# Input products of both feed-forwards of a decoder layer as seven block products each, with the weight block sums formed by GpSimd

## The chip, the cores and the metric

The kernel runs on one core of one Trainium2 chip. The metric is the device time of one execution in microseconds (us); the median of three timed executions of the kernel before is 1368.93 us, with 1367.86 and 1369.23 as lowest and highest.

The engines are named as the profile names them: PE is TensorE (matmuls), PEld its weight load, DVE is VectorE, ACT is ScalarE, POOL is GpSimd, SP is SyncE, which here issues the weight DMAs. SBUF is the memory that the engines work in, PSUM the accumulators that PE writes. Each engine takes its instructions in the order in which they stand in its own queue; a waiting instruction holds up those behind it.

## The reference

One layer for 512 tokens of 1024 features in float32: feed-forward, mixer (state-space heads beside differential attention), cross-attention to a memory, second feed-forward, final norm. The change touches both feed-forwards:

```python
def rms_norm(x, w):
    x32 = x.astype(jnp.float32)
    y = x32 * lax.rsqrt(jnp.mean(x32 * x32, axis=-1, keepdims=True) + EPS)
    return y.astype(x.dtype) * w

def swiglu(h, w_in, w_out):
    gate, up = jnp.split(h @ w_in, 2, axis=-1)
    return (jax.nn.silu(gate) * up) @ w_out

...
        x = x + 0.5 * swiglu(rms_norm(x, norm_ffn1_w[l]), ffn1_w_in[l], ffn1_w_out[l])
...
        x = x + 0.5 * swiglu(rms_norm(x, norm_ffn2_w[l]), ffn2_w_in[l], ffn2_w_out[l])
    return rms_norm(x, norm_final_w)
```

`w_in` is 1024 x 5632: 22 tiles of 128 columns for the gate and 22 for the up part.

## The kernel before

**Layout.** The state `x` lies feature-major: eight tiles `x[k]` of 128 features by 512 tokens. A product's weight tile (128 features by 128 outputs) is PE's stationary operand, the 512 tokens are the moving one, and the sum over the eight feature tiles is taken in one PSUM bank of 128 x 512.

**Three matmuls for one.** Every float32 operand is split into a rounded part and the rest (`hi` and `lo`, type fp32r): ACT writes `hi` (L144), DVE writes `lo = src - hi` (L145). `mm3` then takes hi x hi, hi x lo and lo x hi. A weight tile is thus loaded by `load_w` (L161): a 512 KB DMA into `wr` (128 x 1024, four buffers), ACT's `wh`, DVE's `wl` (three buffers each). At the start the splits of these weights are held by `tc.issue_after` until the splits of the first input tiles have been put in the queues (`start`).

**Feed-forward.** `ffn` (L289) goes through the 22 output tiles in three thirds of 8, 8 and 6. For each tile `ffn_pairs` (L270) makes the gate product `pg` and the up product `pu`, 8 x 3 matmuls each. DVE multiplies `pg` by the norm's row (L308), ACT takes the tanh (L310), DVE finishes the gate (L311) and multiplies by `pu` (L312), and the result is split into `g`. After a third, its `g` tiles go through eight output products `po` and are added to `x`. The first two tile pairs of the first feed-forward are special: `ffn_first` (L279) makes them together, one input tile at a time, as `x` and the first weights `wa` arrive. The norm's own row is ready only after that, and the gates wait for it. The last third of the second feed-forward is closed by token (`Close`, products `pf`), with the final norm; it loads its own weights through the same four `wr` buffers (`Close.weights`).

**What sets the order.** `Order` emits the matmuls: dense work is a queue of generators, and chains of dependent steps are let in after an estimated time (`od.t`). The tile framework's scheduler then sets the order of the queues of PE, DVE, ACT and POOL from this; only SP's queue stands as written. The framework also gives each new tile a free buffer of its pool and adds the waits for its release.

**The middle of the kernel** (mixer and cross-attention) isn't touched. It holds the only stage that runs matmuls of 256 columns back to back with a weight load each: `pck`, the keys of the memory (256 rows), in `memory_keys`.

## Time and profile before

| | us |
|---|---|
| median of three timed executions | 1368.93 |
| the profiled execution, its span | 1368.1 |
| PE busy | 1347.8 |
| DVE busy | 794.1 |
| ACT busy | 537.7 |
| POOL busy | 73.7 |

The profiled execution's own time is its span, 1368.1 us from the first to the last instruction, 0.8 us under the median. Shares and groups are for the whole span; the stages differ. In 60 to 370 us, which is nearly all of the first feed-forward, DVE is busy 153.97 of 310 us, ACT 88.50, POOL 3.08, and PE 310.00. A matmul's time in a row (390 ns for 512 columns) is from its start to the modelled end of its pipeline; the rate is read from the distance of starts, or from a piece of the chain of waits (its length over its count). The same holds in a lesser degree for DVE and ACT: the next instruction starts some 0.08 us ahead of the shown end of the one before.

### The profile page before, as it was taken

How to read it: one execution, taken by the hardware profiler on the slowest of the kernel's cores; microseconds unless marked ns; L12 is line 12 of the kernel's file. 1: busy time of each engine (PE TensorE's matmuls, PEld its weight loads, DVE VectorE, ACT ScalarE, POOL GpSimd, SP SyncE). 2: the span in 40 equal slices, each digit the busy share in tenths (PEclk: the TensorE clock that was granted, in tenths of full speed). 3: DMA queues.
4: the chain of work that ended last, by engine and by line, in shares of the span. 5: the costliest groups of instructions: out<-in, count | busy, mean ns of one | idle time of the engine just before them, and what ended most of it. 6: DMA issues, size and time to landing. Idle time of an engine off the chain costs nothing.

```text
span 1368.1 us, 16518 instructions
## 1 busy us (share of the span) xinstructions
PE 1347.8 (99%) x6457; PEld 1107.6 (81%) x6457; DVE 794.1 (58%) x1302; ACT 537.7 (39%) x958; POOL 73.7 (5%) x92
## 2 busy tenths in 40 slices
PE   8999999999999999999999989999999999999997
PEld 6888888888887788877888868888888888888886
DVE  6644444445786686657777767555654444444543
ACT  5421222223454564446654564343432222221432
POOL 1100000000020001100102111000000000000000
PEclk9999999999999999999999999999999999999999
DMA  6353333322342214432156274221323332332411
GB/s 237 110 164 113 94 93 99 100 92 81 115 154 65 91 47 100 125 91 70 29 142 104 80 148 137 94 63 47 92 93 96 104 94 93 103 112 77 136 50 62
DMA packets 41934, 136.74 MB, mean 100 GB/s; under 512 B 5552, under 2 KB 5960, under 8 KB 41856
## 3 DMA queue, kind: packets, MB, share of 16 engines
q1 hardware_dynamic: 37968, 124.61, 29.1%
q0 software_dynamic: 3888, 11.09, 4.9%
q8 instruction: 50, 0.82, 0.2%
q14 instruction: 28, 0.23, 0.1%
HBM read 133.52 MB, written 4.77 MB: 101 GB/s over the span
## 4 chain that ended last, share of the span: by engine, by line
PE 95%; DMA 1%; issue 1%; POOL 1%; ACT 1%; DVE 1%; SPq 0%; POOLq 0%; ACTq 0%; DVEq 0%
PE pg L135 17%; PE pu L135 17%; PE po L135 16%; PE pm L135 9%; PE pxbc L135 7%; PE pk L135 3%; PE pq L135 3%; PE pz L135 3%; PE pcq L135 3%; PE pv L135 3%; PE pf L135 2%; PE pa L135 2%; PE ps L135 2%; PE pck L135 1%; DMA wr<-in_wcv 1%
## 5 line engine op out<-in xcount | busy, mean ns | idle before, releaser
L144 ACT ACTIVATE wh<-wr 128x1024 fp32r<-128x1024 f32 (+2 forms) x228 | 232.6, 1022 | 546.6 <-issue 311.8
L145 DVE TENSOR_TENSOR wl<-wr,wh 128x1024 fp32r<-128x1024 f32 (+2 forms) x228 | 268.4, 1178 | 73.5 <-ACT wh L144 72.5
L135 PE MATMUL pg<-hmh,wl 128*128 128x512 f32 x336 | 130.9, 390 | 0.5 <-DVE wl L145 0.5
L135 PE MATMUL pg<-hmh,wh 128*128 128x512 f32 x336 | 131.1, 390 | 0.0
L135 PE MATMUL pu<-hmh,wh 128*128 128x512 f32 x336 | 131.0, 390 | 0.0
L135 PE MATMUL pg<-hml,wh 128*128 128x512 f32 x336 | 130.9, 390 | 0.0
L135 PE MATMUL pu<-hml,wh 128*128 128x512 f32 x336 | 130.8, 389 | 0.0
L135 PE MATMUL pu<-hmh,wl 128*128 128x512 f32 x336 | 130.8, 389 | 0.0
L135 PE MATMUL po<-gh,wh 128*128 128x512 f32 x304 | 118.4, 390 | 0.0
L135 PE MATMUL po<-gh,wl 128*128 128x512 f32 x304 | 118.3, 389 | 0.0
L135 PE MATMUL po<-gl,wh 128*128 128x512 f32 x304 | 118.3, 389 | 0.0
L312 DVE TENSOR_TENSOR gate<-pu,gate 128x512 f32<-128x512 f32 x42 | 29.0, 692 | 107.1 <-PE pu L135 107.1
L323 DVE TENSOR_TENSOR upd<-po,row 128x512 f32<-128x512 f32 x40 | 27.7, 692 | 98.3 <-PE po L135 98.2
L308 DVE TENSOR_TENSOR gate<-pg,row 128x512 f32<-128x512 f32 x42 | 29.0, 691 | 94.4 <-PE pg L135 94.4
L135 PEld LDWEIGHTS pg<-hmh,wl 128*128 128x128 f32 x336 | 63.1, 188 | 14.1 <-DVE wl L145 0.9
L135 PEld LDWEIGHTS pu<-hmh,wh 128*128 128x128 f32 x336 | 63.1, 188 | 13.9 <-issue 0.9
L135 PEld LDWEIGHTS pu<-hmh,wl 128*128 128x128 f32 x336 | 63.1, 188 | 13.2
L135 PEld LDWEIGHTS pg<-hmh,wh 128*128 128x128 f32 x336 | 63.1, 188 | 13.0
L135 PEld LDWEIGHTS pu<-hml,wh 128*128 128x128 f32 x336 | 63.1, 188 | 12.9
L135 PEld LDWEIGHTS pg<-hml,wh 128*128 128x128 f32 x336 | 63.1, 188 | 12.9
L135 PEld LDWEIGHTS po<-gh,wl 128*128 128x128 f32 x304 | 57.1, 188 | 12.0
L135 PEld LDWEIGHTS po<-gh,wh 128*128 128x128 f32 x304 | 57.1, 188 | 11.8
(310 smaller groups left out, 2704.8 us busy)
## 6 DMA issues: line engine op xcount, KB each, us to landing
wr<-in_f2i SPq DMA_DIRECT2D x44, 512.0 KB, 3.5
wr<-in_f1i SPq DMA_DIRECT2D x40, 512.0 KB, 3.5
wr<-in_f2o SPq DMA_DIRECT2D x22, 512.0 KB, 3.6
wr<-in_f1o SPq DMA_DIRECT2D x16, 512.0 KB, 3.6
wr<-in_wxbc SPq DMA_DIRECT2D x16, 512.0 KB, 3.6
wr<-in_wck SPq DMA_DIRECT2D x8, 512.0 KB, 3.5
wr<-in_wq SPq DMA_DIRECT2D x8, 512.0 KB, 3.8
wr<-in_wk SPq DMA_DIRECT2D x8, 512.0 KB, 3.5
```

What stands on the lines that cost most here:

```text
L135: nc.tensor.matmul(out, w, x, start=start, stop=stop)
L144: S.activation(hi, src, AF.Copy),
L145: V.tensor_tensor(lo, src, hi.bitcast(F32), ALU.subtract),
L308: V.tensor_tensor(gate, pg, st.row, ALU.mult)
L312: V.tensor_tensor(gate, pu, gate, ALU.mult)
L323: V.tensor_tensor(upd, po, row4, ALU.mult)
```

## The change

Four blocks are taken from the input and four from the weights, and the 2 x 2 block product is made with seven products in place of eight (Strassen's scheme in Winograd's form).

- **Input blocks** are even and odd feature tiles by first and second half of the tokens (`H` = 256 columns). `block_sums` forms the four sums S1 to S4 of a pair of tiles on DVE (two scalings of 512 columns, four sums of 256), then splits them (two ACT, two DVE instructions of 512): once in each feed-forward for each of four pairs.
- **Weight blocks** of a *quad* (two gate tiles and two up tiles): `b11` and `b21` are the gate's even and odd rows, `b12` and `b22` the up part's; each is 128 x 1024, one 512 KB DMA. POOL forms four sums t1 to t4 of them in SBUF (`sum_w`, `wt`, two buffers), and seven operands instead of four go through the ACT and DVE split.
- **Products.** `add_product` makes one block product: two output tiles, four pairs of feature tiles, three matmuls, each of 256 columns: 24 matmuls. A quad has seven: b11, t1, t2, b21, t3, b22, t4.
- **Combination.** Three PSUM banks `qa`, `qe`, `qb` hold the running sums. ACT copies `qa` into `qb` after the first product, keeps `p5` and `u2`; DVE subtracts `u2` from `qe` and makes `c22`. At the end `qa` and `qb` are the gate for the two halves of the tokens, `qe` and `c22` the up part.
- `ffn_quads` turns a quad into two `g` tiles (two gate chains of 512 columns, four multiplications of 256). The first feed-forward has 10 quads behind `ffn_first`, the second 11. A third has 3, 4, 3 and 4, 4, 3 quads.
- Four matmuls on a constant (`init`) are put at the start of PE's queue.
- The weights' layout in HBM is changed to match. Weights of quads are split by `split_w`, which has no `issue_after`.

```diff
+    def block_sums(k0, gain, raw):
+        fe, fo = s2("fe"), s2("fo")
+        V.tensor_scalar(fe, x[k0], par[:, gain + k0 : gain + k0 + 1], None, ALU.mult)
+        V.tensor_scalar(fo, x[k0 + 1], par[:, gain + k0 + 1 : gain + k0 + 2], None, ALU.mult)
+        s12, s34 = s2("s12"), s2("s34")
+        V.tensor_tensor(s12[:, :H], fe[:, H:], fo[:, H:], ALU.subtract)
+        V.tensor_tensor(s34[:, :H], fe[:, :H], fe[:, H:], ALU.subtract)
+        V.tensor_tensor(s12[:, H:], s12[:, :H], fe[:, :H], ALU.subtract)
+        V.tensor_tensor(s34[:, H:], s12[:, H:], fo[:, :H], ALU.add)
+        s12, s34 = split("s12", s12), split("s34", s34)
...
+    def add_product(ps, w, xs, which, first):
+        wh, wl = w
+        n = len(xs)
+        for f in range(2):
+            out = ps[:, f * H : (f + 1) * H]
+            for kp in range(n):
+                wc = slice((f * n + kp) * P, (f * n + kp + 1) * P)
+                xh, xl = xs[kp][which]
+                for j, (a_, b_) in enumerate(((wh, xh), (wh, xl), (wl, xh))):
+                    od.t += (H + 32) / 2400
+                    nc.tensor.matmul(out, a_[:, wc], b_, start=first and f == 0 and kp == 0 and j == 0, stop=kp == n - 1 and j == 2, skip_group_check=True)
+                yield
+
+    def raw_w(src):
+        raw = wp.tile([P, D], F32, tag="wr", name=nm("wr"), bufs=4)
+        nc.sync.dma_start(raw, src)
+        return raw
+
+    def sum_w(a_, b_):
+        t = wp.tile([P, D], F32, tag="wt", name=nm("wt"), bufs=2)
+        G.tensor_tensor(t, a_, b_, ALU.add)
+        return t
+
+    def split_w(raw):
+        hi = wp.tile([P, D], R32, tag="wh", name=nm("wh"))
+        lo = wp.tile([P, D], R32, tag="wl", name=nm("wl"))
+        split_into(hi, lo, raw)
+        return hi, lo
+
+    def quad(xs, src):
+        b12, b11 = raw_w(src[0]), raw_w(src[1])
+        a_ps = acc("qa")
+        yield from add_product(a_ps, split_w(b11), xs, "11", True)
+        t1 = sum_w(b11, b12)
+        e_ps = acc("qe")
+        b_ps = acc("qb")
+        S.activation(b_ps, a_ps, AF.Copy)
+        yield from add_product(e_ps, split_w(t1), xs, S1, True)
+        p5 = s2("p5")
+        S.activation(p5, e_ps, AF.Copy)
+        b22 = raw_w(src[2])
+        t2 = sum_w(t1, b22)
+        yield from add_product(b_ps, split_w(t2), xs, S2, False)
+        u2 = s2("u2")
+        S.activation(u2, b_ps, AF.Copy)
+        V.tensor_tensor(e_ps, e_ps, u2, ALU.subtract)
+        b21 = raw_w(src[3])
+        yield from add_product(a_ps, split_w(b21), xs, "12", False)
+        t3 = sum_w(b12, b22)
+        yield from add_product(b_ps, split_w(t3), xs, S3, False)
+        c22 = s2("c22")
+        V.tensor_tensor(c22, p5, b_ps, ALU.subtract)
+        yield from add_product(e_ps, split_w(b22), xs, S4, False)
+        t4 = sum_w(t2, b21)
+        yield from add_product(b_ps, split_w(t4), xs, "22", False)
+        yield (a_ps, b_ps), (e_ps, c22)
...
+    for _ in range(4):
+        nc.tensor.matmul(acc("init"), ones_r, ones_r[:, None, :].to_broadcast([P, 4, P]), start=True, stop=True)
...
-    def ffn_pairs(h, wi, f0, nf):
-        for f in range(f0, f0 + nf):
-            pg = acc("pg")
-            yield from proj(pg, load_w(wi[f]), h)
-            pu = acc("pu")
-            yield from proj(pu, load_w(wi[NF + f]), h)
-            yield pg, pu
...
+    def ffn_quads(xs, wq, st, nq, g):
+        for _ in range(nq):
+            made = None
+            for made in quad(xs, next(wq)):
+                if made is None:
+                    yield
+            gs, us = made
+            gates = []
+            for i in range(2):
+                row = st.row[:, None, i * H : (i + 1) * H].to_broadcast([P, 2, H])
+                gate = s2("gate")
+                V.tensor_tensor(halves(gate), halves(gs[i]), row, ALU.mult)
+                th = s2("th")
+                S.activation(th, gate, AF.Tanh, scale=0.5)
+                V.scalar_tensor_tensor(gate, th, 1.0, gate, ALU.add, ALU.mult)
+                gates.append(gate)
+            for f in range(2):
+                gf = s2("gf")
+                fs = slice(f * H, (f + 1) * H)
+                for i in range(2):
+                    V.tensor_tensor(gf[:, i * H : (i + 1) * H], us[i][:, fs], gates[i][:, fs], ALU.mult)
+                g.append(split("g", gf))
+            yield
...
             if ti == 0 and first is not None:
-                parts = [ffn_first(h, first), ffn_pairs(h, wi, f0 + 2, nf - 2)]
+                for made in ffn_first(h, first):
+                    if made is None:
+                        yield
+                    else:
+                        g.append(split("g", gated(*made, st.row)))
+                for k0 in range(0, KT, 2):
+                    xs.append(block_sums(k0, C_FFN1, h))
+                nq -= 1
...
     def upd_2(o, po):
         V.tensor_tensor(x[o], x[o], po, ALU.add)
         h_2.append(make_h(o, C_FFN2))
+        if o % 2:
+            xs_2.append(block_sums(o - 1, C_FFN2, h_2))
```

**How the queues stand.** Three places matter below. In the rows a name's last number counts tiles, and the number after the `L` is the line in the kernel whose queue it is.

First, DVE at the start of the first feed-forward, from the gate of the second tile pair of `ffn_first` (`pa`) on. Before, the gate of the next pair (`pg`) follows:

```order
L308 TENSOR_TENSOR gate_67_365<-pa_50_232,row_61_351 128x512
L145 TENSOR_TENSOR wl_90_482<-wr_88_479,wh_89_481 128x1024
L311 SCALAR_TENSOR_TENSOR gate_67_365<-th_68_367,gate_67_365 128x512
L312 TENSOR_TENSOR gate_67_365<-pa_52_234,gate_67_365 128x512
L145 TENSOR_TENSOR gl_70_372<-gate_67_365,gh_69_371 128x512
L308 TENSOR_TENSOR gate_79_437<-pg_71_375,row_61_351 128x512
```

Now the block sums stand there:

```order
L361 TENSOR_TENSOR gate_70_371<-pa_54_240,row_65_359 128x512
L364 SCALAR_TENSOR_TENSOR gate_70_371<-th_71_373,gate_70_371 128x512
L366 TENSOR_TENSOR gate_70_371<-pa_56_242,gate_70_371 128x512
L144 TENSOR_TENSOR wl_128_591<-wt_126_588,wh_127_590 128x1024
L144 TENSOR_TENSOR gl_73_378<-gate_70_371,gh_72_377 128x512
L180 TENSOR_SCALAR fe_74_381<-x0_79,par_77 128x512
L181 TENSOR_SCALAR fo_75_382<-x1_83,par_77 128x512
L183 TENSOR_TENSOR s12_76_385<-fe_74_381,fo_75_382 128x256
L184 TENSOR_TENSOR s34_77_386<-fe_74_381 128x256
L185 TENSOR_TENSOR s12_76_385<-s12_76_385,fe_74_381 128x256
L186 TENSOR_TENSOR s34_77_386<-s12_76_385,fo_75_382 128x256
L144 TENSOR_TENSOR s12l_79_392<-s12_76_385,s12h_78_391 128x512
```

The split of `s34` and three more such groups of eight, for the other pairs of input tiles, come right behind, all ahead of any further weight split.

Second, DVE and ACT where one quad ends and the next is under way. Before, for one output tile, DVE has:

```order
L308 TENSOR_TENSOR gate_199_1168<-pg_191_1106,row_61_351 128x512
L145 TENSOR_TENSOR wl_210_1213<-wr_208_1210,wh_209_1212 128x1024
L311 SCALAR_TENSOR_TENSOR gate_199_1168<-th_200_1170,gate_199_1168 128x512
L312 TENSOR_TENSOR gate_199_1168<-pu_195_1137,gate_199_1168 128x512
L145 TENSOR_TENSOR wl_218_1254<-wr_216_1251,wh_217_1253 128x1024
L145 TENSOR_TENSOR gl_202_1175<-gate_199_1168,gh_201_1174 128x512
```

Now, from the weight split for t1 of the next quad (`wl_354`), with `qb_314`, `qe_313` and `c22_329` from the quad that ends:

```order
L144 TENSOR_TENSOR wl_354_2028<-wt_350_2022,wh_353_2027 128x1024
L383 TENSOR_TENSOR gate_337_1970<-qb_314_1778,row_65_359 128x512
L392 TENSOR_TENSOR gf_339_1975<-qe_313_1777,gate_335_1965 128x256
L144 TENSOR_TENSOR wl_359_2062<-wt_357_2059,wh_358_2061 128x1024
L386 SCALAR_TENSOR_TENSOR gate_337_1970<-th_338_1972,gate_337_1970 128x512
L392 TENSOR_TENSOR gf_339_1975<-c22_329_1905,gate_337_1970 128x256
L144 TENSOR_TENSOR wl_363_2095<-wr_361_2092,wh_362_2094 128x1024
L144 TENSOR_TENSOR gl_341_1979<-gf_339_1975,gh_340_1978 128x512
```

And on ACT at the same place, where `qb_352` is the next quad's accumulator, copied from its `qa_347`:

```order
L385 ACTIVATE th_338_1972<-gate_337_1970 128x512
L143 ACTIVATE wh_362_2094<-wr_361_2092 128x1024
L143 ACTIVATE gh_340_1978<-gf_339_1975 128x512
L237 ACTIVATE qb_352_2025<-qa_347_1993 128x512
L143 ACTIVATE gh_343_1985<-gf_342_1982 128x512
```

The copy into `qb`, on which the next quad's third product rests, stands behind a step of the ended quad's gates.

Third, POOL within the feed-forwards. Before, it has only DMA issues and a few small things there (`mem` is the memory input):

```order
L215 TENSOR_TENSOR ncol_55_326<-nv_54_324,mhalf_120 128x4
L226 TENSOR_TENSOR ndiag_60_348<-ident_111,cl_57_342 128x512
L743 DMA mem_383_2292<-in_memT 128x256
L375 DMA rel_d_224<-rel_far_120_659 8x128
L743 DMA mem_386_2311<-in_memT 128x256
```

Now it has t1 to t4 of one quad, and then t1 and t2 of the next:

```order
L215 TENSOR_TENSOR wt_350_2022<-wr_346_1991,wr_345_1989 128x1024
L215 TENSOR_TENSOR wt_357_2059<-wt_350_2022,wr_356_2057 128x1024
L215 TENSOR_TENSOR wt_364_2122<-wr_345_1989,wr_356_2057 128x1024
L215 TENSOR_TENSOR wt_370_2182<-wt_357_2059,wr_361_2092 128x1024
L215 TENSOR_TENSOR wt_388_2269<-wr_384_2238,wr_383_2236 128x1024
L215 TENSOR_TENSOR wt_395_2306<-wt_388_2269,wr_394_2304 128x1024
```

With two `wt` buffers, t3 is written where t1 lay and so waits for DVE's split of t1, and t4 waits for the split of t2.

More of the change, by code (lines that the diff above doesn't have):

```diff
@@ L1 @@
 from contextlib import ExitStack
-from itertools import chain
 import math
@@ L233, in __init__ @@
             self.acc = None
+            self.row = None
         def add(self, xk):
@@ L938, in finish @@
                 nc.sync.dma_start(a["out"][tb][:, T:], xg[1])
-    od.add(ffn(h_2, st_2, a["f2i"], [a["f2o0"], a["f2o1"]], close=Close()))
+    od.add(ffn(h_2, xs_2, st_2, a["f2q"], [a["f2o0"], a["f2o1"]], close=Close()))
     od.run()
```

59 lines of the change are left out of this document (39 added, 20 removed).

## The prediction

> **What bounds the kernel now.** I read the page's busy line and the shares of the chain of waits first, then the chain in order of time inside the feed-forwards, then the timelines of DVE, ACT and POOL there.
>
> ```profile
> PE 1347.8 (99%) x6457; PEld 1107.6 (81%) x6457; DVE 794.1 (58%) x1302; ACT 537.7 (39%) x958; POOL 73.7 (5%) x92
> PE 95%; DMA 1%; issue 1%; POOL 1%; ACT 1%; DVE 1%; SPq 0%; POOLq 0%; ACTq 0%; DVEq 0%
> 147.50 5.44 PE pu L135 x24
> 380.67 15.60 PE pck L135 x130
> 31.88 0.40 PE L135 MATMUL pg<-hmh,wh 128*128 128x512 f32 x1
> ```
>
> PE is the bound: it has no waits worth naming in the feed-forwards, and the chain stays on it for 95% of the span. So a term counts if it changes PE's work or makes PE wait. The third line gives PE's rate with 512 columns: 5.44 us for 24 matmuls, 226.7 ns each. The fourth gives the rate with 256 columns, a weight load for each: 15.60 over 130, 120.0 ns. Half the columns cost 53% of the time.
>
> **Term 1, PE's work.** Four output tiles (two gate, two up) took 4 x 24 = 96 matmuls of 226.7 ns, 21.76 us. A quad takes 7 x 24 = 168 of 120.0 ns, 20.16 us; one product is 2.88 us. That is 1.60 us less a quad, and 21 quads give **-33.6 us**. One product in eight is saved, but only 7% of the time.
>
> **Term 2, the start of the first feed-forward.** Here the order counts.
>
> ```profile
> 32.08 0.60 ACT L253 ACTIVATE row<-nrow 128x512 f32<-128x512 f32 x1 [9.12 <-PE nrow L135]
> 32.71 0.43 DVE L306 TENSOR_SCALAR row<-row 128x512 f32<-128x512 f32 x1 [2.12 <-ACT row L253]
> 33.05 0.69 DVE L308 TENSOR_TENSOR gate<-pa,row 128x512 f32<-128x512 f32 x1
> 41.73 0.69 DVE L145 TENSOR_TENSOR gl<-gate,gh 128x512 fp32r<-128x512 f32 x1 [0.70 <-ACT gh L144]
> 70.20 0.69 DVE L308 TENSOR_TENSOR gate<-pg,row 128x512 f32<-128x512 f32 x1 [3.35 <-PE pg L135]
> 70.81 1.22 DVE L145 TENSOR_TENSOR wl<-wr,wh 128x1024 fp32r<-128x1024 f32 x1
> 71.94 0.69 DVE L311 SCALAR_TENSOR_TENSOR gate<-th,gate 128x512 f32<-128x512 f32 x1
> 72.55 1.22 DVE L145 TENSOR_TENSOR wl<-wr,wh 128x1024 fp32r<-128x1024 f32 x1
> 378.20 0.42 DVE L759 TENSOR_TENSOR ckf<-pck,row 128x256 f32<-128x256 f32 x1
> 378.54 0.68 DVE L226 TENSOR_TENSOR ndiag<-ident,ch 128x512 fp32r<-128x512 f32 x1
> ```
>
> From the distances of starts DVE's prices are 0.61 us (512 columns, 70.20 to 70.81), 1.13 (1024, 70.81 to 71.94), 0.34 (256, 378.20 to 378.54) and 0.34 for a scaling of 512 (32.71 to 33.05). The block sums stand in DVE's queue behind the gates of `ffn_first`, and these wait for the norm's row, ready at 32.7. In the run before the last step of those gates starts at 41.73 and frees DVE at 42.34; the weight split of t3, now among them, and the row's multiple, now later, make it 42.34 + 1.13 - 0.34 = 43.1. A group costs 2 x 0.34 + 4 x 0.34 + 2 x 0.61 = 3.26, and some 0.25 for ACT's part of the split: 3.5. The fourth pair's S1 and S2 are split after three groups and 0.68 + 1.36 + 0.25 + 0.61 = 2.9 of the fourth, at 43.1 + 10.5 + 2.9 = 56.5. PE could begin the quad at 31.9 (the first `pg`). Until 56.5 it has the products b11 and b21 (5.76) and three quarters of the first output tile of t1 and t2 (18 matmuls, 2.2). It waits 56.5 - 31.9 - 5.8 - 2.2 = 16.6 us. I take **+17**. Bounds: 14 if ACT's part is hidden and the four `init` matmuls bring the first stage forward, 25 if two of POOL's sums fall into the stretch and the first quad's weight splits, which now stand among those of `wa` and wait there for DMA and POOL, hold up `ffn_first` by 3. In the second feed-forward the sums follow each pair of output products of the cross-attention and are covered by them; there I put nothing (3 us if the last pair's is not covered).
>
> ```profile
> 7.02 0.63 PE L135 MATMUL pa<-hmh,wah 128*128 128x512 f32 x1
> 7.44 0.63 PE L135 MATMUL pa<-hml,wah 128*128 128x512 f32 x1
> ...
> 11.21 0.40 PE L135 MATMUL pa<-hml,wah 128*128 128x512 f32 x1
> 11.45 0.39 PE L135 MATMUL pa<-hmh,wal 128*128 128x512 f32 x1
> ```
>
> After the idle time at its start PE runs at 420 ns a matmul, and at 240 from 11.21 us on; the profile's clock row shows 1.00 there all the same. No gap as long as the one forecast occurs later in this trace. The Trainium skill, TensorE: Matmul & The Clock Gate, "Part 1: The HAM clock gate", says that PE falls back to half its clock after an idle window of some 3.4 us and needs as long a busy one to leave it. By that rule the sum would be larger by an estimated 1.7 us for one such gap; without it, by nothing.
>
> **Term 3, POOL's sums and DVE's splits between two quads.** DVE's work per quad is 7 splits of 1.13, eight steps of 0.61 (two gates x row, two gate ends, two `gl`, `qe - u2`, `c22`) and four of 0.34: 14.2 us. It has to share something with POOL:
>
> ```profile
> 378.52 1.60 POOL L226 TENSOR_TENSOR ndiag<-ident,cl 128x512 fp32r<-128x512 f32 x1 [0.63 <-DVE cl L222]
> 379.30 1.10 DVE L145 TENSOR_TENSOR ck<-ckf,ck 128x256 fp32r<-128x256 f32 x1
> 784.10 1.03 POOL L226 TENSOR_TENSOR ndiag<-ident,cl 128x512 fp32r<-128x512 f32 x1 [0.26 <-DVE cl L222]
> 784.40 0.69 DVE L639 TENSOR_TENSOR cbm<-pcb,triq 128x512 f32<-128x512 f32 x1 [0.39 <-PE pcb L135]
> 729.00 1.23 DVE L145 TENSOR_TENSOR wl<-wr,wh 128x1024 fp32r<-128x1024 f32 x1
> 729.20 1.93 POOL L226 TENSOR_TENSOR ndiag<-ident,cl 128x512 fp32r<-128x512 f32 x1 [0.75 <-ACT conv L599]
> 828.15 1.23 DVE L145 TENSOR_TENSOR wl<-wr,wh 128x1024 fp32r<-128x1024 f32 x1 [0.21 <-ACT wh L144]
> 828.72 1.81 POOL L719 TENSOR_TENSOR ysq<-ysq,ysq 128x512 f32<-128x512 f32 x1 [36.91 <-ACT ysq L717]
> 776.22 1.28 POOL L719 TENSOR_TENSOR ysq<-ysq,ysq 128x512 f32<-128x512 f32 x1 [35.37 <-ACT ysq L717]
> ```
>
> At 784.10 POOL takes 1.03 us beside a DVE step of which one input is in PSUM (`pcb`), and neither is slowed. At 729.20 the same POOL operation starts 0.2 us behind a weight split, which reads two tiles of SBUF, and takes 1.93: the split ends at 730.2, and 0.9 follow. At 828.72 it is likewise. At 379.30 it is DVE that waits: 1.10 us for a step of 256 columns (0.42 above), until POOL's 378.52 + 1.60 is over. So a DVE instruction with both inputs in SBUF and a POOL instruction take turns, whole instruction by whole instruction, and a waiting POOL gets in between two DVE instructions.
>
> No row has a POOL sum of 1024 columns. Twice the 1.03 is 2.06, twice the 1.28 is 2.56; the waiting DVE starts a little ahead of POOL's shown end, so I take 2.2. The Trainium skill, GPSIMD Engine Reference, "3.1 Elementwise — side-by-side cycle accounting", gives 4497 ns for an add of 2048 float32 elements, an estimated 2.25 us for 1024; with it this term would be 1 to 2 us larger.
>
> Four sums are 8.8 us a quad beside DVE's 14.2, together 23.0 against PE's 20.16. What PE feels is one path: from the end of the seventh product to the third product of the next quad, which starts from ACT's copy `qb`.
>
> ```profile
> 59.15 1.06 ACT L144 ACTIVATE wh<-wr 128x1024 fp32r<-128x1024 f32 x1 [3.25 <-issue]
> 60.11 0.40 ACT L241 ACTIVATE nsq<-mem 128x256 f32<-128x256 f32 x1
> 60.42 0.61 ACT L310 ACTIVATE th<-gate 128x512 f32<-128x512 f32 x1
> 60.94 0.40 ACT L241 ACTIVATE nsq<-mem 128x256 f32<-128x256 f32 x1
> ```
>
> ACT's prices are 0.96 (1024) and 0.52 (512). The path on DVE: gate x row 0.61, `gf` 0.34, split of t2 1.13, gate end 0.61, `gf` 0.34; then ACT's `gh` 0.52 and the copy 0.52: 4.1 us, while PE has two products, 5.76. The slack is 1.7. POOL's t3 waits only for the split of t1, just ahead of this path, and t4 for the split of t2, within it. Of t3's 2.2 us some 0.95 pass beside the first two steps, which read PSUM; 1.25 delay the split. t4 delays the second `gf` by 2.2. With 0.4 for seven handovers, PE waits 1.25 + 2.2 + 0.4 - 1.7 = 2.2 us. POOL's t2 can come ahead of the path and hold up the split of t1, since b22's buffer is free only after the ended quad's sixth split: up to 1 us more. I take 2.6. There are 15 places where a quad follows a quad in a third (2 + 3 + 2 and 3 + 3 + 2): **+39**. Lower bound 0, if the turns fall beside idle times of DVE; upper bound (14.2 + 4 x 2.56 - 20.16) x 15 = 64, if nothing overlaps.
>
> The Trainium skill, SBUF — State Buffer, "Who interferes with whom", speaks against this change: an instruction of DVE with two SBUF inputs contends with a GpSimd instruction that reads SBUF, by an exclusive lock for the whole instruction. The rows above agree. If the two shared bandwidth instead, 0.2 us of overlap at 729 would have cost some tenths and not 0.9, and this term would be near its lower bound.
>
> **Term 4, buffers in the last third.** `Close.weights` takes two of the four `wr` buffers at each quad's end.
>
> ```profile
> wr<-in_f1i SPq DMA_DIRECT2D x40, 512.0 KB, 3.5
> ```
>
> b22 of the next quad then gets the buffer of its own b11 and waits for t1; b21 gets b12's and waits for t3. From t2 on: t3 2.2, b21's DMA 3.5, split 2.1 (0.96 + 1.13), 7.8 us to the fourth product, in which PE has t2's split and the third product, 2.1 + 2.88 = 5.0. 2.8 us late, in two quads: **+6** (0 if the sums run ahead, 12 if b22's own wait adds as much).
>
> **Term 5, the ends of the thirds.** Behind the last product now stand 0.61 + 0.34 + 1.13 + 0.61 + 0.34 + 0.52 + 0.61 = 4.2 us to the first new `g` tile and 1.8 more to the second; before it was 0.61 + 0.52 + 0.61 = 1.7. The output products have 6 ready tiles of 18 matmuls (4.1 us) in four thirds and 4 of them (2.7) in two, with a few matmuls of the next output put between. Late by up to 1.2 in four and 2.6 in two, 10 in all; I take **+7** (0 to 10).
>
> **The sum** is -33.6 + 17 + 39 + 6 + 7 = +35. The profiled execution spans 1368.1 us, 0.8 under the median of 1368.93; on the median it gives **1404 us**, 2.6% slower.
>
> **Rivals.** (a) *The turns cost PE nothing*: the sums and splits find room in DVE's and POOL's idle times, and term 3 is 0. For it: 14.2 + 8.8 us need not be serial, as the row at 784.40 shows, and scheduling leaves slack of 1.7 us on the path. Against it: three rows of whole waits, and t3 and t4 wait for splits on that very path. It gives 1368.93 - 33.6 + 17 + 6 + 7 = 1365; the point from which it decides is 0.24 us of wait in each of the 15 places (3.6 / 15), below which the kernel isn't slower. If the start also costs its lower bound, 1362. (b) *DVE and POOL become the bound throughout*: nothing overlaps, a quad takes 14.2 + 4 x 2.56 = 24.4 us, 4.3 over PE's, in all 21 quads: +90 - 33.6 + 17 + 13 = +86, 1455. For it: the path has five steps of DVE behind one another; against it: the one-input steps run beside POOL. (c) *The change doesn't save what it says*: 256 columns take more than 120 ns here. Break-even on PE alone is 21.76 / 168 = 129.5 ns; then term 1 is 0 and the sum 1438. Against it: 130 matmuls of `pck` with the same order of hi and lo.
>
> **Chances.** Forecast 0.66 (own range 1380 to 1436), (a) 0.18, (b) 0.12, (c) 0.04. The range 1362 to 1438 leaves out (b), (c) and the lower part of (a). A measurement of this kernel tells about 0.2% from no change, 2.7 us: (a) at 1365 lies at that limit, so I split it, 0.12 faster and 0.06 about the same, and the forecast's lowest end adds 0.01 to the latter; slower has 0.81.
>
> **What would show it.** Term 1: rows of `qa`, `qb`, `qe` 120 ns apart, PE's distance within a product 2.88 us. Term 2: PE idle between about 35 and 56 us, released by DVE's `s12l`. Term 3: in steady quads PE waits before the first matmul of t2's product, released by ACT's `qb`; POOL rows of `wt` well over 2.2 us where they start behind a `wl`, and `wl` rows of over 2 us where POOL is first. Term 4: PE waits in the last third for splits of b22 and b21, behind late DMAs. The forecast is wrong if the quads run at 20.2 us each, or if DVE has no idle time at all in them.

## The result, and the profile after

The changed kernel takes **1432.23 us** (median of four executions, 1431.15 to 1433.64) against 1368.55 of the kernel before on the same chip: ratio 1.0464, 95% interval 1.0449 to 1.0479. It is 4.6% slower, where 1404 (2.6% slower) was forecast. The profiled execution spans 1431.3 us, 63.2 more than before's 1368.1.

The busy line and the shares of the chain of waits, from the page of the changed kernel:

```profile
PE 1346.7 (94%) x7973; PEld 1170.1 (82%) x7973; DVE 1041.7 (73%) x1513; ACT 645.4 (45%) x1100; POOL 291.7 (20%) x176
PE 3%; DMA 2%; DVE 1%; issue 1%; POOL 1%; ACT 1%; POOLq 0%; ACTq 0%; DVEq 0%; SPq 0%
```

The chain of waits no longer stays on PE for 95% of the span: from its end back it soon leaves PE, so it explains the last stages only. The stages have to be compared one by one. First the kernel before, then the changed one, by the view of busy times in windows: from and to, length, then busy time and instruction count of PE, PEld, DVE, ACT and POOL, PE's granted clock, DMA share and GB/s. The rows are: the start up to the first pair or quad; the rest of the first third; the second and the last third of the first feed-forward; the three thirds of the second; output products are left out.

```profile
0.00:31.88 31.88, 26.16 (x107) 21.21 (x108) 20.43 (x35) 19.13 (x29) 4.37 (x13) 1.00 0.71 250
31.88:98.38 66.50, 66.50 (x292) 54.08 (x291) 36.63 (x56) 23.89 (x36) 6.98 (x12) 1.00 0.42 129
141.90:228.94 87.04, 87.04 (x386) 72.08 (x385) 40.31 (x48) 24.74 (x31) 0.00 (x0) 1.00 0.32 98
272.46:337.74 65.28, 65.28 (x290) 54.06 (x289) 32.08 (x42) 20.68 (x29) 0.00 (x0) 1.00 0.27 86
994.00:1083.29 89.29, 88.96 (x396) 73.23 (x394) 42.67 (x55) 26.60 (x34) 2.34 (x2) 1.00 0.31 95
1126.81:1213.85 87.04, 87.04 (x386) 72.10 (x384) 40.31 (x48) 24.81 (x31) 0.00 (x0) 1.00 0.31 98
1259.67:1327.29 67.62, 67.14 (x303) 55.25 (x302) 34.87 (x44) 26.21 (x39) 0.00 (x0) 1.00 0.35 109
```

```profile
0.00:42.86 42.86, 31.60 (x110) 23.56 (x111) 26.00 (x35) 18.82 (x29) 12.32 (x15) 0.92 0.49 173
42.86:137.79 94.93, 72.84 (x511) 68.49 (x510) 76.52 (x107) 40.97 (x60) 32.42 (x23) 0.84 0.23 74
181.45:271.52 90.07, 84.11 (x676) 82.79 (x674) 79.44 (x71) 43.95 (x55) 37.09 (x14) 0.98 0.29 94
315.17:378.32 63.15, 61.18 (x506) 60.64 (x504) 55.57 (x55) 32.81 (x43) 23.41 (x9) 1.00 0.27 90
1036.66:1132.40 95.74, 86.27 (x684) 83.97 (x682) 88.56 (x90) 46.69 (x60) 38.14 (x16) 0.98 0.27 89
1176.06:1261.48 85.42, 81.77 (x673) 80.88 (x672) 75.67 (x70) 42.73 (x53) 33.90 (x13) 1.00 0.30 99
1307.00:1391.26 84.26, 70.00 (x531) 67.65 (x531) 56.71 (x57) 36.28 (x52) 25.58 (x10) 0.94 0.27 88
```

Together these stages are 494.65 us before and 556.43 after: 61.8 of the 63.2 lie in them. Compare each with its quads alone, 20.16 us apiece: 60.48 for three, 80.64 for four. The thirds that follow another third are nearest to that (63.15 for 60.48, 85.42 and 90.07 for 80.64); the rest of the first third takes 94.93 for 60.48, and the very last third 84.26 for 60.48. Before, PE is busy from edge to edge of nearly all these stages; after, DVE is busy for up to 93% of a stage. And the clock column, 1.00 in all stages before, falls to 0.84.

**The start.** In the timeline (start, duration, instruction, idle time before it and what ended that), of POOL, DVE, PE and ACT of the changed kernel:

```profile
25.80 2.76 POOL L215 TENSOR_TENSOR wt<-wr,wr 128x1024 f32<-128x1024 f32 x1 [1.83 <-DVE wl L144]
54.93 2.72 POOL L215 TENSOR_TENSOR wt<-wt,wr 128x1024 f32<-128x1024 f32 x1 [12.45 <-DVE wl L144]
...
19.29 2.48 DVE L144 TENSOR_TENSOR wl<-wr,wh 128x1024 fp32r<-128x1024 f32 x1 [6.84 <-ACT wh L143]
21.69 2.83 DVE L144 TENSOR_TENSOR wal<-wa,wah 128x512 fp32r<-128x512 f32 x1
...
55.37 2.56 DVE L180 TENSOR_SCALAR fe<-x,par 128x512 f32<-128x512 f32 x1
...
63.44 0.48 DVE L180 TENSOR_SCALAR fe<-x,par 128x512 f32<-128x512 f32 x1
...
24.58 0.79 PE L134 MATMUL pa<-hmh,wal 128*128 128x512 f32 x1 [4.02 <-DVE wal L144]
25.17 0.63 PE L134 MATMUL pa<-hmh,wah 128*128 128x512 f32 x1
25.60 0.63 PE L134 MATMUL pa<-hml,wah 128*128 128x512 f32 x1
62.25 0.58 PE L205 MATMUL qe<-s12h,wh 128*128 128x256 f32 x1 [9.72 <-ACT s12h L143]
73.99 0.58 PE L205 MATMUL qe<-s12h,wh 128*128 128x256 f32 x1 [1.97 <-ACT s12h L143]
...
43.06 0.60 ACT L342 ACTIVATE row<-nrow 128x512 f32<-128x512 f32 x1 [11.05 <-PE nrow L134]
```

Three weight splits (`wl`) of the first quad stand on DVE among the splits of `wa`; the first waits 6.84 us for its ACT half, which waits for a DMA, and then all take turns with POOL's sums. A split of `wa` (`wal`, 0.68 us elsewhere) takes 2.83 and PE waits 4.02 for it. The norm's row is ready at 43.06, 11 us later than before, and gates and block sums follow it. `fe` takes 2.56 us beside POOL's sum (54.93), as does `fo` behind it beside the next sum; without a sum `fe` takes 0.48. PE waits 9.72 us for the first S1, S2, and gets the fourth pair's only at 73.99.

**A steady quad.** Around the handover at 1217 us, where a quad's seventh product ends, POOL, DVE, ACT and PE:

```profile
1213.58 2.40 POOL L215 TENSOR_TENSOR wt<-wt,wr 128x1024 f32<-128x1024 f32 x1 [1.22 <-DVE wl L144]
1218.95 2.41 POOL L215 TENSOR_TENSOR wt<-wr,wr 128x1024 f32<-128x1024 f32 x1 [2.97 <-DVE wl L144]
1228.87 2.40 POOL L215 TENSOR_TENSOR wt<-wt,wr 128x1024 f32<-128x1024 f32 x1 [7.50 <-DVE wl L144]
...
1214.57 2.50 DVE L144 TENSOR_TENSOR wl<-wr,wh 128x1024 fp32r<-128x1024 f32 x1
1217.60 1.21 DVE L144 TENSOR_TENSOR wl<-wt,wh 128x1024 fp32r<-128x1024 f32 x1
1218.73 0.68 DVE L383 TENSOR_TENSOR gate<-qb,row 128x512 f32<-128x512 f32 x1
1219.66 2.79 DVE L144 TENSOR_TENSOR wl<-wt,wh 128x1024 fp32r<-128x1024 f32 x1
...
1224.08 0.58 ACT L237 ACTIVATE qb<-qa 128x512 f32<-128x512 f32 x1
...
1224.71 0.39 PE L205 MATMUL qb<-s12h,wh 128*128 128x256 f32 x1 [1.67 <-ACT qb L237]
```

POOL's sum of t2 (1213.58) holds up the split behind the first gate step (2.50 us for 1.22). So the split of t1 (1217.60) comes only when the seventh product has ended, and the second gate step (1218.73) waits behind it; the sum of t3 (1218.95) holds up the split of t2 for 1.57 us more than the 1.22 that it takes alone. The copy `qb` comes 1.7 us late, and PE waits before the third product.

**The last third.** SP's queue from 1300 to 1395 us (line, what its DMA issue waited for, us in total, times, longest):

```profile
SPq L210 <- POOL wt L215: 22.0, 3, 8.2
...
SPq L1030 <- POOL wt L215: 13.2, 3, 7.6
```

PE's and ACT's rows in the timeline, in the second of the three quads (`wfh` are the splits of output weights):

```profile
1350.97 0.58 PE L205 MATMUL qb<-s34h,wh 128*128 128x256 f32 x1 [5.37 <-ACT u L245]
...
1345.99 1.13 ACT L143 ACTIVATE wfh<-wr 128x512 fp32r<-128x512 f32 x2
1347.42 1.06 ACT L143 ACTIVATE wh<-wt 128x1024 fp32r<-128x1024 f32 x1 [0.29 <-POOL wt L215]
...
1350.29 0.62 ACT L245 ACTIVATE u<-qb 128x512 f32<-128x512 f32 x1
```

L1030 is `Close.weights`, L210 a quad's own blocks. Both wait for POOL's sums to release a `wr` buffer, and for DVE's splits as well (18.8 and 16.0 us), and blocks arrive late: ACT waits 6.58 us for the next quad's b11, until 1357.49. But PE's longest stop, 5.37 us, is not a late block. The quad's fifth product needs ACT's copy `u` of `qb`, and on ACT `u` stands behind four splits of output weights and the split of t4. PE's waits in this third are 7.1 us for `u`, 3.0 for the copy `qb` and 4.2 for weight splits (`wl` 3.2, `wh` 1.0).

### The profile page after: what moved, and what is told of

Its sections match the earlier page's. It is cut to its first block, busy times and chain, and to the rows that moved or that the text cites. A ratio compares the mean times of both kernels' runs of the same rounds, so it can differ in the third digit from the quotient of the medians.

```text
span 1431.3 us, 20180 instructions
## 1 busy us (share of the span) xinstructions
PE 1346.7 (94%) x7973; PEld 1170.1 (82%) x7973; DVE 1041.7 (73%) x1513; ACT 645.4 (45%) x1100; POOL 291.7 (20%) x176
## 5 line engine op out<-in xcount | busy, mean ns | idle before, releaser
L215 POOL TENSOR_TENSOR wt<-wr,wr 128x1024 f32<-128x1024 f32 x42 | 113.9, 2712 | 340.4 <-DMA wr<-in_f2q 166.7
L144 DVE TENSOR_TENSOR wl<-wt,wh 128x1024 fp32r<-128x1024 f32 x84 | 142.5, 1698 | 20.8 <-ACT wh L143 20.6
L215 POOL TENSOR_TENSOR wt<-wt,wr 128x1024 f32<-128x1024 f32 x42 | 104.5, 2487 | 211.5 <-DVE wl L144 180.2
L143 ACT ACTIVATE wh<-wt 128x1024 fp32r<-128x1024 f32 x84 | 88.6, 1056 | 103.6 <-POOL wt L215 39.5
L205 PE MATMUL qa<-hmh,wh 128*128 128x256 f32 x336 | 97.4, 290 | 3.1 <-ACT qb L237 2.1
L205 PE MATMUL qa<-hml,wh 128*128 128x256 f32 x336 | 97.2, 289 | 3.1 <-DVE hml L148 3.1
L205 PE MATMUL qa<-hmh,wl 128*128 128x256 f32 x336 | 97.4, 290 | 2.6 <-DVE wl L144 2.6
L205 PEld LDWEIGHTS qa<-hmh,wh 128*128 128x128 f32 x336 | 66.5, 198 | 3.6 <-ACT qb L237 2.3
L205 PEld LDWEIGHTS qa<-hml,wh 128*128 128x128 f32 x336 | 66.5, 198 | 3.5 <-DVE hml L148 3.3
L205 PEld LDWEIGHTS qa<-hmh,wl 128*128 128x128 f32 x336 | 66.5, 198 | 3.2 <-DVE wl L144 3.2
```

The source lines that it names most:

```text
L143: S.activation(hi, src, AF.Copy),
L144: V.tensor_tensor(lo, src, hi.bitcast(F32), ALU.subtract),
L205: nc.tensor.matmul(out, a_[:, wc], b_, start=first and f == 0 and kp == 0 and j == 0, stop=kp == n - 1 and j == 2, skip_group_check=True)
L215: G.tensor_tensor(t, a_, b_, ALU.add)
```

## The experiments

Each ratio is to the kernel before, run on the same chip, with its 95% interval. Edits are to the changed kernel unless another is named.

**1. `start_gate`: the weight splits held until the splits of `wa` are out.**

```diff
 def split_w(raw):
-        split_into(hi, lo, raw)
+        with ExitStack() as after:
+            for i in start:
+                after.enter_context(tc.issue_after(i))
+            split_into(hi, lo, raw)
```

> The weight splits of the quads now wait, as those of load_w do, until the last split of wa has been issued. Theory (three splits of the first quad stand among the splits of wa and hold ffn_first up while they wait for POOL): the 96 products of ffn_first end at 32 to 34 us instead of 42.9, the norm's row, the gates and the block sums come as much earlier, and the whole is 8 to 11 us shorter, 1421 to 1424. Rival (the first quad needs POOL's four sums and DVE's block sums one after another anyway, so only the wait changes its place): ffn_first ends early, but the first output product po starts where it did, and the time changes by less than 4 us.

1424.59 us, ratio 1.0417 (1.0386 to 1.0447), 0.5% under the changed kernel's. The products of `ffn_first` end at 35.4 us (42.1 in the changed kernel), later than the 32 to 34 expected; the first quad starts at 36.73 instead of 42.86, the first `po` at 131.97 instead of 137.79. The theory holds for the place; the gain, some 6 us, lies between the two expectations.

**2. `start_early`: also the block sums ahead of the gates.**

```diff
     for k in range(KT):
         st1.add(x[k])
+    xs_1 = [block_sums(k0, C_FFN1, h1) for k0 in range(0, KT, 2)]
...
-    for k0 in range(0, KT, 2):
-        xs.append(block_sums(k0, C_FFN1, h))
```

> As start_gate, and the block sums of the first feed-forward are made before ffn_first's gates are, so that DVE does them while PE runs ffn_first and the norm. Theory (block sums behind the gates keep PE waiting in the first quad): the wait of qe for s12h, 15.6 us in all, falls under 4, the first output product po starts 20 to 28 us earlier than in the changed kernel, and the time is 1403 to 1412. Rival (DVE's and POOL's work in the first 60 us is the bound, in whatever order): less than 5 us better than start_gate.

1420.30 us, 1.0385 (1.0355 to 1.0415). The first `po` comes at 129.11, only 2.9 us earlier than in `start_gate`: the rival is right. PE's waits from 25 to 130 us say where the time stays:

```profile
PE qb L205 <- ACT u L248: 7.7, 1, 7.7
PE qb L205 <- ACT qb L240: 4.7, 1, 4.7
PE nrow L134 <- DVE ndiag L317: 4.0, 1, 4.0
```

The wait of `qe` for `s12h` is gone, and three others stand in its place: the norm's row now queues behind the block sums on DVE, and the gates behind it.

**3. `no_sums`: POOL's sums left out.**

```diff
-        t1 = sum_w(b11, b12)
-        yield from add_product(e_ps, split_w(t1), xs, S1, True)
+        yield from add_product(e_ps, split_w(b11), xs, S1, True)
```

and t2, t3, t4 likewise.

> The four sums of weight blocks are left out and the products of t1 to t4 take b11, b22, b12 and b21 in their place; everything else stays. Theory (POOL's sums cost PE about 2.1 us in each of 15 places, and most of the lateness of the last third and some of the first quad's): a quad in the middle thirds takes 20.2 to 20.5 us against 20.9 to 22.3, the time is 1380 to 1396. Rival (PE waits between quads for PSUM or for the gates' chain, not for POOL): quads stay over 21.3 us and the time is over 1410.

1381.04 us, 1.0098 (1.0069 to 1.0127): 51 us of the 64 go with the sums. Quads in the middle thirds start 20.16 us apart. What remains over PE's own time: 27 us in the first third (87.66 for 60.48) and 18 in the last (78.53), where one quad still waits 5.1 us for a late block.

**4. `unread_sums`: the sums are formed, and nobody waits for them.**

```diff
-        yield from add_product(e_ps, split_w(t1), xs, S1, True)
+        yield from add_product(e_ps, split_w(b11), xs, S1, True)
...
         t2 = sum_w(t1, b22)
-        yield from add_product(b_ps, split_w(t2), xs, S2, False)
+        yield from add_product(b_ps, split_w(b22), xs, S2, False)
```

and the other two products likewise; all four sums stay.

> POOL forms the four sums as before, but no split reads them: the products of t1 to t4 take b11, b22, b12 and b21. What is left of the waits then comes from DVE and POOL taking turns (and from buffers that the sums hold), what goes was waiting for a sum. Theory (turns): rows of wl keep a mean of 1.4 us and more, quads in the middle thirds take 21.3 to 22.2 us, and the time is at most 12 us below the changed kernel's 1432, wherever the start is left aside. Rival (PE waits for the sums themselves, and the turns are hidden): quads take 20.2 to 20.5 us, within 0.2 of those without sums, and the time is within 5 us of that run.

1471.40 us, 1.0759 (1.0728 to 1.0790). The rival (PE waits for the sums themselves) falls: with nobody reading them, quads behind another quad in the two second thirds take 22.9 to 24.8 us, and in the second of these thirds PE's waits are for DVE's `gate` (5.9 us) and ACT's copy `qb` (1.7), none for a sum or a DMA. But our number falls too, since the time is 39 us *above* the changed kernel's. DVE and POOL at a handover between two quads:

```profile
1242.42 3.27 POOL L215 TENSOR_TENSOR wt<-wt,wr 128x1024 f32<-128x1024 f32 x1
1245.77 2.74 POOL L215 TENSOR_TENSOR wt<-wr,wr 128x1024 f32<-128x1024 f32 x1
...
1243.35 2.90 DVE L386 SCALAR_TENSOR_TENSOR gate<-th,gate 128x512 f32<-128x512 f32 x1
1246.17 3.43 DVE L144 TENSOR_TENSOR wl<-wr,wh 128x1024 fp32r<-128x1024 f32 x1
```

Four sums follow one another right there (the first starts at 1238.92, the last at 1248.59), one between every two steps of DVE that read SBUF twice. In the changed kernel the sums wait for splits to free their buffers, which spreads them over the quad. So the price of a turn depends on where it falls. Part of the price is PE's rate: 264 matmuls of 256 columns start 211 to 216 ns apart here, against 123 in the changed kernel, in place of 120. That is an estimated 13 of the 39 us at most (see the clock, below).

**5. `dve_sums`: the sums on DVE.**

```diff
-        G.tensor_tensor(t, a_, b_, ALU.add)
+        V.tensor_tensor(t, a_, b_, ALU.add)
```

> DVE forms the four sums of weight blocks instead of POOL; all else as in the changed kernel. DVE then has 14.2 + 4 x 1.13 = 18.7 us of work for a quad, and no instruction of POOL to take turns with. Theory (the turns are the cost): rows of wl come back to 1.2 to 1.3 us, quads in the middle thirds take 20.2 to 21.0 us against 22.2, and the time is 1398 to 1418. Rival (DVE itself is the narrow place between two quads, whoever forms the sums): quads stay at 22 us or more and the time is over 1425.

1384.10 us, 1.0115 (1.0092 to 1.0139), **48 us less for one letter**, and below the expected range. Groups of DVE (count, busy us, mean ns of one, idle time before):

```profile
L144 DVE TENSOR_TENSOR wl<-wt,wh 128x1024 fp32r<-128x1024 f32 x84 | 103.4, 1232 | 16.1 <-ACT wh L143 15.7
L215 DVE TENSOR_TENSOR wt<-wr,wr 128x1024 f32<-128x1024 f32 x42 | 51.4, 1223 | 10.6 <-DMA wr<-in_f1q 7.3 <-DMA wr<-in_f2q 2.6
```

The window of the first feed-forward's second third, columns as above:

```profile
173.46:254.20 80.74, 80.74 (x674) 80.74 (x673) 71.19 (x83) 42.95 (x53) 0.00 (x0) 1.00 0.32 105
```

The same group in the changed kernel:

```profile
L144 DVE TENSOR_TENSOR wl<-wt,wh 128x1024 fp32r<-128x1024 f32 x84 | 142.5, 1698 | 20.8 <-ACT wh L143 20.6
```

The splits of sums fall from 1698 to 1232 ns; the sum itself takes DVE 1.22 us and POOL 2.4. DVE is busy for 71 of 81 us, and PE has no gap at all in it: four quads in 80.74 us.

**6. `late_wf`: output weights of the last third loaded in mid-quad.**

```diff
-                if at_end and close is not None:
+                if at_end and close is not None and (i % 57 == 36 or i == 57 * nq - 1):
                     while close.n < len(g):
                         close.weights(close.n)
```

`i` counts the generator's steps, 57 in a quad; step 36 is behind the sum t3.

> In the last third of the second feed-forward the two tiles of output weights of a quad are loaded in the middle of the next quad's products, not at the quad's end, so b22 and b21 of the next quad no longer wait for the buffers of their own b11 and b12. Theory (buffers of wr make the last third late): its three quads take 63 to 72 us instead of 84.3, and the time is 1414 to 1421. Rival (the turns of POOL and DVE, with the transposes' copies among them, make it late): the last third loses less than 5 us.

1419.26 us, 1.0372 (1.0351 to 1.0393). The last third takes 70.73 us instead of 84.26, with POOL's sums still there: place and size are as expected. Why is less clear, for the edit moves the splits of the output weights with their loads. In this third SP still waits 38.1 us for POOL's sums (35.2 in the changed kernel), and ACT still waits up to 5.67 us for a block. What is gone is PE's wait for `u`. So in the changed kernel it was ACT's queue and not a late block that stopped PE longest. No run moves the loads without the splits.

**7. `plain_first`: the first quad without Strassen**, on top of `start_early`.

```diff
+    def plain_quad(h, src):
+        b12, b11, b22, b21 = (raw_w(src[i]) for i in range(4))
+        for even, odd in ((b11, b21), (b12, b22)):
+            w = split_w(even), split_w(odd)
+            for f in range(2):
+                p_ = acc("qp")
+                for k in range(KT):
+                    wc = slice((f * 4 + k // 2) * P, (f * 4 + k // 2 + 1) * P)
+                    mm3(p_, w[k % 2], h[k], k == 0, k == KT - 1, wc=wc)
```

> As start_early, and the first quad of the first feed-forward is computed with eight block products in plain order (96 products of 512 columns, 21.8 us, no block sums, no sums of weights). Theory (the first quad waits for DVE's block sums, 14 us of work that PE has nothing to cover with): the first output product po starts at 99 to 106 us against 129 in start_early, and the time is 1391 to 1400. Rival (DVE's and POOL's work up to there is too much in any order): the two quads behind it wait in its place, and the time is over 1408.

1404.25 us, 1.0263 (1.0242 to 1.0283). The first `po` comes at 117.97: 11 us gained on `start_early` where 23 to 30 were expected. PE still waits 6.4 us for the row's `ndiag` behind the block sums. The time lies between the two expectations: the quad covers part of the sums' work.

**8. `all_fixes`: 1, 2, 5, 6 and a plain first quad in both feed-forwards.**

> Everything together: weight splits of the start gated, block sums early, the first quad of each feed-forward in plain order, output weights of the last third loaded late, sums of weights on DVE. Theory: PE saves 19 x 1.6 = 30 us and gives back some 8 in places between quads, 3 at the start, 7 at the ends of thirds and 3 in the last third: 1350 to 1366, at or below the kernel before. Rival (18.7 us of DVE work a quad leaves too little room, so PE waits 1.5 us and more in each place): over 1375.

**1355.93 us**, ratio 0.9899 (0.9879 to 0.9919): 1% faster than the kernel before, inside the expected range. Quads of the two second thirds take 20.15 to 20.26 us, the last third 64.70. PE's longest wait is at the start (25 to 112 us):

```profile
PE nrow L134 <- DVE ndiag L331: 6.8, 1, 6.8
```

**9. `sums_later`: all_fixes with the block sums behind the gates again.**

> As all_fixes, with the block sums of the first feed-forward back in their place behind ffn_first's gates; the first quad in plain order covers them. In all_fixes PE waited 6.8 us for the norm's row, whose ndiag stood behind the block sums on DVE. Theory (that wait is the sums' place on DVE, and a plain quad of 21.8 us covers 14 us of sums): the wait for ndiag falls under 1.5 us, the first output product po starts at 101 to 106 us against 111.3, and the time is 1344 to 1352. Rival (the sums then come too late for the second quad, which waits in the row's place): po starts at 109 or later, and the time is within 3 us of all_fixes.

1358.44 us, 0.9918 (0.9905 to 0.9932). The row's wait falls to 1.7 us, and a new one of 9.0 comes in its place:

```profile
PE qa L205 <- DVE gate L378: 9.0, 1, 9.0
```

The plain quad's gates stand behind the block sums, and `qa` of the next quad needs their PSUM buffer. The rival is right: `po` at 112.81, and the time 2.5 us from that of `all_fixes`.

**10. `sums_later_pool`: the same with the sums on POOL.**

> As sums_later, with the sums of weight blocks on POOL as in the changed kernel. Theory (DVE and POOL taking turns costs PE some 2 us in each quad, with the start and the buffers mended too): 22 to 45 us more than sums_later, 1370 to 1392, slower than the kernel before. Rival (the turns hurt only because the start and the buffers were late): at most 12 us more than sums_later.

1396.20 us, 1.0200 (1.0182 to 1.0219), 37.8 us more than `sums_later`, as expected (the time itself is over the expected 1392, since `sums_later` came out over its own range): with the start and the buffers mended, POOL's sums alone turn a gain of 0.8% into a loss of 2%. Over 19 quads that is 2.0 us each.

**11. `no_init`: sums_later without the `init` matmuls.**

> As sums_later, without the four init matmuls at the start. Theory (they only run PE for 2 us before the first tiles arrive, and 11 instead of 13 of the first matmuls take 427 ns): 0 to 1.5 us more than sums_later. Rival (they spare the whole slow stretch): 2.5 us more and over.

1360.49 us, 0.9939 (0.9921 to 0.9957), 2.0 more than `sums_later`, between the two expectations; the intervals overlap. PE's first matmuls come 427 ns apart until 10.1 us. With `init` that ends at 9.6 in `sums_later` and at 10.0 in the changed kernel, and over all runs with it between 8.5 (`all_fixes`) and 12.3 (`plain_first`). That `init` is worth anything isn't shown.

**12. `sums_split`: half of the block sums early, half behind the gates.**

> As sums_later, with the first two groups of block sums made early, as in all_fixes, and the last two behind ffn_first's gates. In all_fixes the whole 14 us stood ahead of the norm's row, in sums_later ahead of the plain quad's gates, which then held PE up for 9.0 us over a buffer. Theory (half of the sums at each place lets both pass): the row's ndiag waits less than 3 us, the buffer's wait is under 3 us, the first output product po starts at 101 to 107 us against 111.3 and 112.8, and the time is 1345 to 1352. Rival (DVE's work up to there is too much for any order): po at 110 or later, the time within 3 us of all_fixes.

1356.34 us, 0.9915 (0.9902 to 0.9929). The waits fall from 9.0 and 6.8 us, and neither goes (from 25 to 120 us):

```profile
PE qa L205 <- DVE gate L378: 5.8, 1, 5.8
PE nrow L134 <- DVE ndiag L331: 3.1, 1, 3.1
```

`po` starts at 108.47, against 111.3 and 112.8: between the two expectations, with the rival's time. From 20 to 110 us DVE is busy for 75.97 of 90 us here. The three versions 8, 9 and 12 can't be told apart by their times.

## Why the prediction was right in its sign and 28 us short

Stage lengths in us; the last column but one sums the seven stages, the last is the rest of the span.

| | start | 1st third | 2nd | 3rd | 1st third | 2nd | 3rd | sum | rest |
|---|---|---|---|---|---|---|---|---|---|
| before | 31.88 | 66.50 | 87.04 | 65.28 | 89.29 | 87.04 | 67.62 | 494.7 | 873.5 |
| changed | 42.86 | 94.93 | 90.07 | 63.15 | 95.74 | 85.42 | 84.26 | 556.4 | 874.9 |
| no_sums | 36.23 | 87.66 | 80.87 | 60.47 | 85.13 | 80.63 | 78.53 | 509.5 | 869.2 |
| dve_sums | 41.92 | 87.85 | 80.74 | 60.59 | 85.88 | 81.23 | 75.15 | 513.4 | 866.7 |
| all_fixes | 30.04 | 81.29 | 80.74 | 60.78 | 84.79 | 80.63 | 64.70 | 483.0 | 873.2 |

Of the changed kernel's 63.2 us, term by term (excess over 20.16 us a quad, less what the same stage had over 21.76 a pair of pairs before):

| term | predicted | measured |
|---|---|---|
| 1, PE's work | -33.6 | -33.6 |
| 2, start and first quad | +17 | +38 |
| 3, quad behind quad, outside the last third (13 places) | +34 of the 39 | +24 |
| first quads of the other thirds | 0 | +12 |
| 4, last third (with its two places of term 3) | +11 | +21 |
| 5, ends of thirds | +7 | 0 |
| rest | 0 | +1 |

The sum is nearer than its terms: four rows came out 44 us dearer than predicted, and terms 3 and 5 were taken 17 us too dear, which hides part of it. That is luck.

**Term 1 held.** Matmuls of 256 columns run 120 ns apart, a quad without waits takes 20.16 us in `no_sums`, `dve_sums` and `all_fixes`. Rival (c) is out.

**Term 2 was the step that failed, by 21 us** (42.86 - 31.88 for the later start, 90.33 - 42.86 - 20.16 = 27.3 in the first quad). The prediction let `ffn_first` end on time and the row come at 32.7; "the first quad's weight splits ... hold up `ffn_first` by 3" was its upper bound. The row came at 43.06. Three splits without `issue_after` were in DVE's queue ahead of `wa`'s, waiting for a DMA and for POOL. `start_gate` gives 6 of these 11 us back; in it the norm's additions on DVE still take turns with the sums. From there on, along the predicted chain, `ffn_first`'s gates take 1.6 us longer up to the first `fe` (55.37 - 43.69 = 11.7 for 10.1). The block sums take 19.2 us to the fourth S1, S2 for 13.4; 4.2 of these 5.8 us are their first two steps, 2.56 each for 0.48 beside POOL's sums, which the prediction costed as one-input steps without turns. Behind that PE loses 3.2 us more: 1.6 in a wait for the copy `u`, 1.5 by half its rate (the clock, below). DVE is busy for 72.62 of the 90 us from 20 to 110, for 48.59 before. `start_early`, `sums_later` and `sums_split` move the wait between the row, the gates and S1, and none removes it. The prediction followed one chain and did not add up DVE's whole work to the first `po`. That a start with fewer steps on DVE would come further fits these runs, but was not tried.

**Term 3: the mechanism is shown, its size was predicted at 2.6 us a place and is 1.8.** The rows at 1217 us are the predicted path with the predicted end: PE waits before the third product, released by `qb`. One of its parts was wrong: t4 was said to delay the second `gf` by 2.2, but t4 (1228.87) comes when the path is over. In its place stands t2, whose turn pushes the split of t1 into the path, a case that the prediction named with "up to 1 us more". `unread_sums` shows that taking turns alone is enough, `dve_sums` that without POOL it is gone, `sums_later_pool` that it costs 2.0 us a quad elsewhere unchanged. Rival (a) (turns cost nothing) was wrong in each of these. Rival (b) (everything serial, 24.4 us a quad) didn't come about in the changed kernel, where the quads that follow another in a third take 20.9 to 24.0 us outside the last third; `unread_sums` comes to the same length (up to 24.8), but with a share of PE's rate in it. The Trainium skill, SBUF — State Buffer, "Who interferes with whom", has an exclusive lock for the whole instruction, and the rows agree: 2.79 us for a split of 1.22 beside a sum of 2.41.

**First quads of thirds** were put at nothing. The one of the second feed-forward takes 30.0 us. Without POOL's sums (`no_sums`, `dve_sums`) it takes 24.6, of which some 2.3 are the norm's, as before, and POOL adds 5.4. Of the 2 us left in `dve_sums`, PE waits 0.9 for the row's `ndiag` on DVE and 0.5 for the copy `qb`; a wait for the block sums themselves ("3 us if the last pair's is not covered") doesn't show there. The first quad of the first feed-forward's second third takes 24.6 too, and 20.3 to 20.4 without POOL's sums: the prediction had no term for POOL at the first quad of a later third.

**Term 4: half the size, and only part of the path.** The late blocks are there as predicted, and SP waits 22.0 and 13.2 us for POOL's sums to release buffers. But PE's waits for weight splits are 4.2 us in this third, and 10.1 are for ACT's copies `u` and `qb`: the prediction followed the buffers and left out ACT, where the splits of output weights stand ahead of `u`. `late_wf` takes 13.5 us out of that third by moving the loads and the splits of two output tiles a quad; which of the two counts for how much stays open.

**Term 5 was nothing.** A stage of output products takes 43.7 us from the end of the quads to the next third (137.79 to 181.45), 43.5 before (98.38 to 141.90): the longer chain was covered, by the ready `g` tiles as far as one can tell.

**The clock.** After each of its five waits of 3 us and more (4.02, 9.72, 4.57, 3.07 and 5.37 us) PE runs at half rate for a while in the changed kernel. From 24.58 on it takes 427 ns a matmul of 512 columns (the rows at 25.17 and 25.60), and the window row has the clock at 0.50:

```profile
24.60:30.30 5.70, 5.46 (x12) 3.78 (x12) 5.70 (x5) 5.70 (x11) 2.76 (x1) 0.50 0.12 35
62.00:90.00 28.00, 20.27 (x118) 18.29 (x119) 20.50 (x40) 10.63 (x17) 5.48 (x6) 0.70 0.17 54
```

Twelve matmuls lose 2.4 us there. From 62.25 the bursts between the block sums run at 213 ns a matmul (12 of them from 75.10 to 77.66) and leave that rate only at 78.5. The bursts up to 73.99 end in a wait for DVE in any case; the 16 matmuls behind it lose 1.5 us. The prediction left open whether a gap is followed by half a clock or by nothing: it is half a clock. The Trainium skill, TensorE: Matmul & The Clock Gate, "Part 1: The HAM clock gate", puts it behind idle windows of some 3.4 us; here it also follows waits of 3.07 us (1041.09) and 2.08 us (47.98, 13 matmuls), though not one of 2.43 us (38.21).

Over the whole span the changed kernel has 123 matmuls of 256 columns and 32 of 512 at half rate, the kernel before 14 and 19. At 0.093 and 0.2 us each that is an estimated 13 of the 63 us, and less where such a burst ends in a wait. Part of what the waits cost is thus paid behind them.

## What to carry to other kernels

Saving PE's work moves the bound: a scheme that trades one product in eight for sums has to find those sums a place on an engine with room, and a slower idle engine isn't room where its instructions lock the busy one out; 48 us went with one letter. Count the whole work of the next engine from the start to each point at which PE needs its result; if it doesn't fit, changing its order only moves the wait, and leaving the scheme out for one quad is cheaper. Side work that shares a pool of buffers and an engine's queue, as the output weights do here, belongs where both have room, not where its data are first known.

## What the runs showed of the hardware that was not expected

- A DVE instruction with one tensor in SBUF can take turns with POOL as well: the scaling `fe` takes 2.56 us beside a sum and 0.48 without. The prediction had only instructions with two SBUF inputs do so. (The Trainium skill, SBUF — State Buffer, "Who interferes with whom", lists `tensor_scalar` in its two-port modes among those that take the shared pair; the row agrees.)
- The same sum of 128x1024 takes POOL 2.40 us with nothing beside it and DVE 1.22.
- Sums that nobody reads cost more (1471.40 us) than sums that are read (1432.23): unread they come four in a row, and PE runs more matmuls at half rate (264 of 256 columns against 123).
